# Two transformer blocks on one core: the delta rule's preparation beside the last convolution and the gate, its recurrence beside the indexer's projections

## The chip, the core and the metric

The kernel runs on one core of one Trainium2 chip. The metric is device time in microseconds (us) of one execution. Names of engines: TensorE (PE, with its weight loads as PEld) multiplies matrices, the vector engine (DVE), the scalar engine (ACT) and GpSimd (POOL) work on elements, and SyncE (SP) issues the transfers.

## The reference, cut to what matters

Two layers of a first block, then two layers of a second. The change lies in the first block's attention: a gated delta rule over chunks of 64 tokens in 4 heads, beside sparse attention whose keys are picked by an indexer.

```python
def first_block(x, meta_tokens, w_in, conv_w, a_log, ...):
    h = concatenate([meta, x], axis=1)                  # 16 + 256 tokens, width 1024
    for l in range(DEPTH):                              # DEPTH = 2
        proj = h @ w_in[l]
        dq, dk, dv, dz, db, da, sq, sk, sv, iq, ik, iw = split(proj, SPLIT_POINTS, axis=-1)
        o_dn = deltanet_group(dq, dk, dv, dz, db, da, conv_w[l], ...)
        o_sa = dsa_group(sq, sk, sv, iq, ik, iw, cos, sin, cos_i, sin_i, k_top)
        mix = concatenate([o_dn, o_sa], axis=-1) @ w_out[l]
        ...                                             # layer norm, mixture of experts, layer norm

def deltanet_group(q, k, v, z, b_logit, a_logit, conv_w, a_log, dt_bias, norm_g):
    qkv = silu(causal_dwconv(concatenate([q, k, v], -1), conv_w))
    q, k = l2norm(q), l2norm(k)
    o = chunk_gated_delta_rule(q, k, v, g, beta)
    return o * rsqrt(mean(o * o, -1) + 1e-6) * norm_g * silu(z)

def chunk_gated_delta_rule(q, k, v, g, beta):           # chunks of 64 tokens
    tmat = triangular_solve(eye + lower, eye)           # lower: strict part of k k^T, decayed
    u, w = tmat @ (v * beta), tmat @ (k * beta * exp(gc))
    def step(state, inp):                               # one chunk after the other
        v_new = u_n - w_n @ state
        o_n = qd_n @ state + a_n @ v_new
        return state * exp(gl_n) + kd_n^T @ v_new, o_n

def dsa_group(q, k, v, qi, ki, wi, ...):
    qi, ki = apply_rope(qi), apply_rope(ki)             # the indexer's projections
    score = einsum(relu(qi @ ki^T), wi)
    _, sel = top_k(score, k_top)                        # then attention over the chosen keys
```

## The kernel before

The 272 tokens stand as columns, features as partitions. A projection takes blocks of 128 weight columns: SP fetches two blocks at a time into a ring of four 1 MB buffers, ACT rounds a block to `wh` (line 237), DVE (every fourth time POOL) forms the rest `wl` (line 238), and TensorE makes 24 products of 128x272 for it (lines 245 to 247), into one of three `ps_d` banks. Such a block is called a projection block below.

In each of the two layers `b1_attention` runs, in program order: four projection blocks each for k, q and v with a convolution behind each block (`conv`: one ACT product, three DVE sums of line 395, one tanh, one DVE product of line 398); `squares` and `norms` for the l2 norms; the delta rule's preparation `Delta.pre` for three token tiles t = 2, 0, 1 (16, 128 and 128 tokens), taken in turns by `interleave`; four projection blocks of the gate `zs`; the recurrence `Delta.run` over the tiles; then one block for the indexer's keys `ikT` and four for its queries `iqT`, each with a rotation (`rope`); and then the attention's own projections with the indexer's scores.

`norms` computes the reciprocal roots `rr`: DVE scales the sums of squares (lines 416, 417), POOL raises them to the power -1/2 (line 418), DVE scales again (419, 420). The preparation's first products read `rr` (line 999). It then inverts a triangular matrix by doubling: five levels (three for the 16 tokens), each with a product `LT` by `Tm`, a mask on DVE (`Z`, line 1071), and products that update `Tm` and `U` on DVE (lines 1076, 1077); each product is 8 matmuls of 64x64 (line 1007). The recurrence has for each chunk `wT` by state (line 1144), `u` on DVE (1145), `qd` by state (1148), `kd` by `u` (1154) and the new state on POOL and DVE (1156, 1157). A tile's output is then normed: ACT squares, DVE sums (1169, 1170), POOL takes the power (1171), DVE multiplies (1173), TensorE transposes (1176).

The program is not run in the order of its lines. A scheduler reads the program order as a priority and lays out one fixed sequence for each engine; an engine then works its sequence off in that order, and an instruction that waits holds those behind it. So the gate's blocks already stood among the preparation's products, and the indexer's among the recurrence's.

Of the kernel before, what the change touches and what calls it, by code (L numbers as in the profile page):

```python
# [8 lines left out]
F32 = mybir.dt.float32  # L9
# [4 lines left out]
OP = mybir.AluOpType  # L14
# [3 lines left out]
T1 = 272  # L18
# [328 lines left out]
def interleave(gens):  # L347

    gens = list(gens)
    while gens:  # L350
        for g in list(gens):
            try:
                next(g)
            except StopIteration:
                gens.remove(g)


def yield_from(gen):

    while True:  # L360
        try:
            next(gen)
        except StopIteration as e:
            return e.value


def b1_attention(K, l, mix, st):
# [13 lines left out]
        return ps[:, :T1]  # L381


    def conv(nm, o, tag, *more):
        x = p.tile([128, 4, T1], F32, name=nm + "T", tag=tag)
        for b in range(2):
            wt = K.first.pop(0) if K.first else wcols(K, w, o + 256 * b)
            for j in range(2):
# [7 lines left out]
                th = p.tile([128, T1], F32, name="cvt", bufs=2)  # L396
                S.activation(th, a, AF.Tanh, scale=0.5)
                K.anchor = V.scalar_tensor_tensor(x[:, ci, :], th, 1.0, a, op0=OP.add, op1=OP.mult)
                for at, f in more:
                    if at == ci:  # L400
                        f()
        return x


    def squares(i, x, hs):
        for h in hs:
            sq = p.tile([128, T1], F32, name="l2sq", tag="irel", bufs=3)
            S.activation(sq, x[:, h, :], AF.Square)
            for t in range(3):
                P = TP[t]  # L410
                PE.matmul(pss[:P, t * 8 + i * 4 + h:t * 8 + i * 4 + h + 1], sq[:, TOFF[t]:TOFF[t] + P],
                          c["one"][:, 0:1], start=True, stop=True)
# [6 lines left out]
        V.tensor_scalar(rr[:, :, 0:4], rr[:, :, 0:4], 0.5, None, op0=OP.mult)  # L419
        V.tensor_scalar(rr[:, :, 4:8], rr[:, :, 4:8], 0.5 * 128 ** -0.5, None, op0=OP.mult)  # L420

    kT = conv("k", 512, "kT")

    wsm = p.tile([128, 8, 16], F32, name="wsm", tag="ikT")
    wv = w.rearrange("(k p) n -> p k n", p=128)
# [42 lines left out]

    rr = p.tile([128, 3, 8], F32, name="rr")
    pss = bank(K, "p")  # L470
    hs = [range(2 * i, 2 * i + 2) for i in range(2)]
    qT = conv("q", 0, "qT", *[(1 + i, lambda i=i: squares(0, kT, hs[i])) for i in range(2)])
    load_consts(K, K.pd, 2, nc.sync)
    vT = conv("v", 1024, "vT", *[(i, lambda i=i: squares(1, qT, hs[i])) for i in range(2)], (1, norms))

    load_consts(K, p, 1, nc.sync)
    if l == 0:
# [2 lines left out]
    for i in range(2):  # L480
        nc.sync.dma_start(wik[:, :, i, :], wv[:, :, 4104:4168])
    dt = [Delta(K, l, t, kT, qT, vT, rr, beta, g) for t in range(3)]
    interleave(dt[t].pre() for t in (2, 0, 1))

    zs = p.tile([128, 4, T1], F32, name="zs", tag="kT")
    for b in range(2):
        wt = wcols(K, w, 1536 + 256 * b)
        for j in range(2):
            ps = ws(wt, j * 128)
            th = p.tile([128, T1], F32, name="cvt", bufs=2)  # L490
            S.activation(th, ps, AF.Tanh, scale=0.5)
            V.scalar_tensor_tensor(zs[:, 2 * b + j, :], th, 1.0, ps, op0=OP.add, op1=OP.mult)


    state = None
    for t in (2, 0, 1):
        state = yield_from(dt[t].run(state, zs, mix, t in tiles))
    st["delta"].close()
    K.wb = st["ring"].enter_context(K.tc.tile_pool(name="wringb%d" % l, bufs=RB, side="right"))
    pa = K.pa = st["delta"].enter_context(K.tc.tile_pool(name="attr%d" % l, bufs=1, side="right"))  # L500


    def rope(ps, dst, scale=None):
        raw = p.tile([128, T1], F32, name="rraw", bufs=2)
# [8 lines left out]
        V.tensor_tensor(t2, pr[:, :T1], c["sin"], op=OP.mult)  # L513
        G.tensor_tensor(dst, dst, t2, op=OP.add)

    K.router = router_weights(K, l, K.hp)
    ikT = p.tile([128, T1], F32, name="ikT", tag="ikT")
    rope(ws(wik.rearrange("p k a n -> p k (a n)"), 0), ikT)
    iqT = p.tile([128, 4, T1], F32, name="iqT")
    for b in range(2):  # L520
        wt = wcols(K, w, 3592 + 256 * b)
        for j in range(2):
            rope(ws(wt, j * 128), iqT[:, 2 * b + j, :])
    bias = {2: K.cbmb}
    sqT = p.tile([128, 4, T1], F32, name="sqT", tag="qT")
    skT = p.tile([128, 4, T1], F32, name="skT", tag="vT")
# [1819 lines left out]
```

## Time and profile before

| What | us |
|---|---|
| median of 3 runs | 2074.73 (2064.63 to 2081.65) |
| the profiled execution's own time | 2060.35 |
| its span, from first to last instruction | 2058.5 |
| TensorE busy in the span | 1939.4 (94%) |
| DVE busy | 1067.2 (52%) |
| ACT busy | 768.2 (37%) |
| POOL busy | 364.8 (18%) |
| granted TensorE clock, mean share of 2.4 GHz | 0.969 |

Matmuls are pipelined and their ends are modelled: a matmul of 128x272 is shown with 0.29 us although one starts every 0.125 us, so the idle time of TensorE that the profile shows is a lower bound. The changed part lies in the first layer at about 50 to 170 us of the span and in the second at about 582 to 700 us.

### The profile page before, as it was taken

How to read it: one execution, taken by the hardware profiler on the slowest of the kernel's cores; microseconds unless marked ns; L12 is line 12 of the kernel's file. 1: busy time of each engine (PE TensorE's matmuls, PEld its weight loads, DVE VectorE, ACT ScalarE, POOL GpSimd, SP SyncE). 2: the span in 40 equal slices, each digit the busy share in tenths (PEclk: the TensorE clock that was granted, in tenths of full speed). 3: DMA queues.
4: the chain of work that ended last, by engine and by line, in shares of the span. 5: the costliest groups of instructions: out<-in, count | busy, mean ns of one | idle time of the engine just before them, and what ended most of it. 6: DMA issues, size and time to landing. Idle time of an engine off the chain costs nothing. (4 is left out here: it accounts for less than half of the span.)

```text
span 2058.5 us, 36224 instructions
## 1 busy us (share of the span) xinstructions
PE 1939.4 (94%) x14910; PEld 1526.9 (74%) x14910; DVE 1067.2 (52%) x2112; ACT 768.2 (37%) x1471; POOL 364.8 (18%) x382
## 2 busy tenths in 40 slices
PE   8999999999799998999779999999999999999999
PEld 7888755544588875544358698989888879898987
DVE  6557545322675664322166755555546675555544
ACT  4323432111341343211055344455435434445543
POOL 1325100000122620000010301314200130132410
PEclk9999989999899999999989999999999999999999
DMA  7213279999531346999953442445555244254453
GB/s 227 86 42 122 105 287 383 421 422 422 195 93 63 117 171 274 407 420 423 416 187 124 143 134 93 159 148 164 187 192 160 82 156 152 83 185 144 165 197 110
DMA packets 199339, 414.67 MB, mean 201 GB/s; under 512 B 26024, under 2 KB 147442, under 8 KB 174594
## 3 DMA queue, kind: packets, MB, share of 16 engines
q1 hardware_dynamic: 192230, 410.52, 54.9%
q8 instruction: 119, 1.95, 0.4%
q10 hardware_dynamic: 6940, 1.78, 0.4%
q14 instruction: 50, 0.41, 0.1%
HBM read 411.23 MB, written 1.05 MB: 200 GB/s over the span
## 5 line engine op out<-in xcount | busy, mean ns | idle before, releaser
L238 DVE TENSOR_TENSOR wl<-w,wh 128x1024 fp32r<-128x1024 f32 x329 | 413.0, 1258 | 260.9 <-ACT wh L237 257.5
L237 ACT CAST wh<-w 128x1024 fp32r<-128x1024 f32 x350 | 365.2, 1046 | 424.4 <-PE ps_d L246 251.9
L245 PE MATMUL ps_d<-hh,wh 128*128 128x256 f32 (+1 forms) x1632 | 481.6, 296 | 5.0 <-ACT wh L237 1.9
L247 PE MATMUL ps_d<-hh,wl 128*128 128x256 f32 (+1 forms) x1632 | 476.3, 292 | 0.2
L246 PE MATMUL ps_d<-hl,wh 128*128 128x256 f32 (+1 forms) x1632 | 474.1, 291 | 1.2 <-DVE hl L253 1.2
L245 PEld LDWEIGHTS ps_d<-hh,wh 128*128 128x128 f32 x1632 | 309.4, 190 | 17.3 <-issue 6.7
L247 PEld LDWEIGHTS ps_d<-hh,wl 128*128 128x128 f32 x1632 | 309.9, 190 | 10.1 <-DVE wl L238 6.8
L246 PEld LDWEIGHTS ps_d<-hl,wh 128*128 128x128 f32 x1632 | 309.5, 190 | 6.3 <-DVE hl L253 1.6
L1288 PE MATMUL ps_d<-wb,hg 128*32 128x256 f32 x1600 | 121.2, 389 | 6.3 <-DMA wb<-in_w 6.3
L2313 POOL TENSOR_TENSOR relu<-relu 128x256 f32<-128x256 f32 x64 | 86.7, 1355 | 129.5 <-ACT relu L2312 129.5
L1288 PEld LDWEIGHTS ps_d<-wb,hg 128*32 128x32 f32 x1600 | 59.4, 112 | 50.8 <-DMA wb<-in_w 9.8
L1320 DVE TENSOR_TENSOR yacc<-yacc,ps_c 128x512 f32<-128x512 f32 x56 | 38.5, 688 | 87.7 <-PE ps_c L1317 87.7
L1276 PE MATMUL ps_c<-oh,yp 128*128 128x128 f32 (+1 forms) x640 | 81.4, 280 | 0.0
L1276 PEld LDWEIGHTS ps_c<-oh,yp 128*128 128x128 f32 (+1 forms) x640 | 75.4, 191 | 7.9 <-issue 5.4
L1308 PE MATMUL ps_d<-wb,hid 128*32 128x512 f32 x400 | 70.4, 665 | 6.9 <-ACT hid L1302 6.8
L2267 POOL TENSOR_TENSOR mergedT<-mergedT,tg 128x256 f32<-128x256 f32 x32 | 32.6, 1039 | 231.7 <-DVE tg L2265 231.7
L238 POOL TENSOR_TENSOR wl<-w,wh 128x1024 fp32r<-128x1024 f32 x21 | 50.3, 2395 | 125.6 <-ACT wh L237 116.0
L1292 DVE SCALAR_TENSOR_TENSOR mth<-mth,ps_d 128x256 f32<-128x256 f32 x16 | 6.7, 421 | 125.1 <-ACT mth L1291 125.1
L1291 ACT ACTIVATE mth<-ps_d 128x256 f32<-128x256 f32 x16 | 6.1, 383 | 165.8 <-PE ps_d L1288 165.8
L1317 PE MATMUL ps_c<-ysl,ohT 128*128 128x512 f32 (+1 forms) x140 | 64.9, 603 | 0.0
L2314 ACT CAST hid<-relu 128x256 fp32r<-128x256 f32 x64 | 26.0, 406 | 92.3 <-POOL relu L2313 92.3
L2315 DVE TENSOR_TENSOR hid<-relu,hid 128x256 fp32r<-128x256 f32 x64 | 27.2, 426 | 58.5 <-ACT hid L2314 58.5
(697 smaller groups left out, 3626.9 us busy)
## 6 DMA issues: line engine op xcount, KB each, us to landing
wb<-in_w SPq DMA_DIRECT2D x150, 1024.0 KB, 14.7
w<-in_w_in SPq DMA_DIRECT2D x82, 1024.0 KB, 5.3
w<-in_w SPq DMA_DIRECT2D x42, 1024.0 KB, 19.7
w<-in_w_up SPq DMA_DIRECT2D x32, 1024.0 KB, 5.1
w<-in_w_down SPq DMA_DIRECT2D x32, 1024.0 KB, 4.8
w<-in_w_out SPq DMA_DIRECT2D x16, 1024.0 KB, 4.9
w<-in_w_branch SPq DMA_DIRECT2D x24, 512.0 KB, 3.5
w<-in_cmp_w SPq DMA_DIRECT2D x8, 1024.0 KB
```

The costliest lines, as they stand in the source:

```text
L237: K.nc.scalar.copy(h, x)
L238: eng.tensor_tensor(lo, x, h.bitcast(F32), op=OP.subtract)
L245: PE.matmul(out, a[0], b[0], start=start, stop=False, skip_group_check=True)
L246: PE.matmul(out, a[0], b[1], start=False, stop=False, skip_group_check=True)
L247: return PE.matmul(out, a[1], b[0], start=False, stop=stop, skip_group_check=True)
L1276: PE.matmul(ps[:, (k % 4) * 128:(k % 4) * 128 + 128], K.yp[t][:P, k * 128:(k + 1) * 128], oh[:P, t, :], start=(k == 4 * kk and t == ts[0] ...
L1288: PE.matmul(pu[j * 32:j * 32 + 32, i * 256:i * 256 + 256], hg[:, k, j * 32:j * 32 + 32], wts[i][j][:, k, :], start=(k == 0 and i == 0), st ...
L1308: PE.matmul(ps[q * 32:q * 32 + 32, :], hid[:, j, q * 32:q * 32 + 32], w2t[q][:, j, hf * 512:(hf + 1) * 512], start=(j == 0), stop=(j == 1) ...
L1317: PE.matmul(ps[rows[t]], ohT[:, off:off + P], ysl[:, hf * 512:(hf + 1) * 512], start=True, stop=True)
L1320: V.tensor_tensor(sl, sl, ps[rows[t]], op=OP.add)
L2267: G.tensor_tensor(m, m, tg, op=OP.add)
L2313: G.tensor_tensor(r, r, r, op=OP.mult)
```

## The change

`conv` is split into the tile's creation and a generator `conv_blocks`, which stops after every block. Only the first block of v is projected ahead of the squares of q and of `norms`; the other three and the gate's four then take turns with the preparation, one block for two rounds of it (`weave(..., 2, 1)`; a round is one step of every tile still in work). The recurrence takes turns with the indexer's five projection blocks in the same way. The router's weights are prepared behind the recurrence and not ahead of it. No operation is added or taken away.

```diff
@@ interleave
                 gens.remove(g)
+        yield
@@ b1_attention
-    def conv(nm, o, tag, *more):
+    def conv(nm, o, tag):
         x = p.tile([128, 4, T1], F32, name=nm + "T", tag=tag)
+        return x, conv_blocks(x, o)
+
+    def conv_blocks(x, o):
...
                 K.anchor = V.scalar_tensor_tensor(x[:, ci, :], th, 1.0, a, op0=OP.add, op1=OP.mult)
-                for at, f in more:
-                    if at == ci:
-                        f()
-        return x
+                yield
...
-    qT = conv("q", 0, "qT", *[(1 + i, lambda i=i: squares(0, kT, hs[i])) for i in range(2)])
+    qT, blocks = conv("q", 0, "qT")
+    for i in range(4):
+        next(blocks)
+        if i in (1, 2):
+            squares(0, kT, range(2 * i - 2, 2 * i))
     load_consts(K, K.pd, 2, nc.sync)
-    vT = conv("v", 1024, "vT", *[(i, lambda i=i: squares(1, qT, hs[i])) for i in range(2)], (1, norms))
+    vT, blocks = conv("v", 1024, "vT")
+    next(blocks)
+    squares(1, qT, range(4))
+    norms()
...
-    interleave(dt[t].pre() for t in (2, 0, 1))
-
-    zs = p.tile([128, 4, T1], F32, name="zs", tag="kT")
-    for b in range(2):
...
-    state = None
-    for t in (2, 0, 1):
-        state = yield_from(dt[t].run(state, zs, mix, t in tiles))
...
+    def gate(zs):
+        for b in range(2):
...
+                V.scalar_tensor_tensor(zs[:, 2 * b + j, :], th, 1.0, ps, op0=OP.add, op1=OP.mult)
+                yield
...
+    def index_keys():
+        rope(ws(wik.rearrange("p k a n -> p k (a n)"), 0), ikT)
+        yield
+        for b in range(2):
+            wt = wcols(K, w, 3592 + 256 * b)
+            for j in range(2):
+                rope(ws(wt, j * 128), iqT[:, 2 * b + j, :])
+                yield
+
+    def chunks():
+        state = None
+        for t in (2, 0, 1):
+            state = yield from dt[t].run(state, zs, mix, t in tiles)
+
+    pre = interleave(dt[t].pre() for t in (2, 0, 1))
+    next(pre)
+    next(pre)
+    zs = p.tile([128, 4, T1], F32, name="zs", tag="kT")
+    weave(pre, chain(blocks, gate(zs)), 2, 1)
+    iqT = p.tile([128, 4, T1], F32, name="iqT")
+    ikT = p.tile([128, T1], F32, name="ikT", tag="ikT")
+    weave(chunks(), index_keys(), 2, 1)
...
     K.router = router_weights(K, l, K.hp)
```

What it does to the sequences is seen at three places; the line numbers of the changed kernel are 1 to 19 higher than before.

First, TensorE in layer 0, from the last product of the squares (`l2sq`) to the first that reads `rr`. Before, where the first left-out stretch holds 45 more projection products, and the second the last eleven of them among small products:

```order
L411 MATMUL ps_p<-cst_94,l2sq 16x1
L245 MATMUL ps_d<-hh,wh 128x272
L246 MATMUL ps_d<-hl,wh 128x272
L247 MATMUL ps_d<-hh,wl 128x272
...
L316 MATMUL ps_c<-cst_94,rows 128x68
L976 MATMUL ps_c<-g,cst_94 16x4
...
L999 MATMUL ps_c<-cst_94,rr 128x16 x4
```

Now, where the left-out stretch holds eight more products of the same three kinds:

```order
L412 MATMUL ps_p<-cst_94,l2sq 16x1
L247 MATMUL ps_d<-hh,wl 128x272
L245 MATMUL ps_d<-hh,wh 128x272
L246 MATMUL ps_d<-hl,wh 128x272
...
L1018 MATMUL ps_c<-cst_94,rr 128x16 x7
```

Between the two stood 59 projection products; now there are 11 (in layer 1: 40 before and 9 now).

Second, DVE in layer 0 in the preparation's first two levels (the last figure in `Z_0`, `Tm_1` is the tile t). Before:

```order
L1071 TENSOR_TENSOR Z_2_969<-ps_c_1039,cst2_572 16x64
L1071 TENSOR_TENSOR Z_0_979<-ps_c_1045,cst2_572 128x256
L1071 TENSOR_TENSOR Z_1_996<-ps_c_1055,cst2_572 128x256
L1076 TENSOR_TENSOR Tm_2_970<-Tm_2_970,ps_c_1070 16x64
L1077 TENSOR_TENSOR U_2_971<-U_2_971,ps_c_1065 16x64
```

Now:

```order
L1080 TENSOR_TENSOR Z_0_904<-ps_c_909,cst2_572 128x256
L399 SCALAR_TENSOR_TENSOR cva_995<-ps_d_970,fcol_157,cva_995 128x270
L1080 TENSOR_TENSOR Z_1_921<-ps_c_926,cst2_572 128x256
L399 SCALAR_TENSOR_TENSOR cva_995<-ps_d_970,fcol_157,cva_995 128x269
L238 TENSOR_TENSOR wl_1199<-w_1196,wh_1198 128x1024
L402 SCALAR_TENSOR_TENSOR vT_574<-cvt_1000,cva_995 128x272
L1090 TENSOR_TENSOR Z_2_894<-ps_c_1003,cst2_572 16x64
L1090 TENSOR_TENSOR Z_0_904<-ps_c_1009,cst2_572 128x256
L1090 TENSOR_TENSOR Z_1_921<-ps_c_1019,cst2_572 128x256
L238 TENSOR_TENSOR wl_1303<-w_1196,wh_1302 128x1024
```

Convolution sums and weight splits now stand among the masks and updates of the levels; before, the convolutions were over by then.

Third, POOL in layer 0 around the first whole tile's output norm (`dnst` is the mean square, `iqT` the indexer's queries). Before:

```order
L1156 TENSOR_TENSOR state_1686<-state_1643,ex1_795 128x512
L512 TENSOR_TENSOR iqT_1789<-rraw_1821,cst1_753 128x272
L514 TENSOR_TENSOR iqT_1789<-iqT_1789,rt2_1825 128x272
L1171 TENSOR_TENSOR dnst_1654<-dnst_1654,nhalf_155 128x4
L512 TENSOR_TENSOR iqT_1789<-rraw_1858,cst1_753 128x272
```

Now:

```order
L511 TENSOR_TENSOR iqT_1581<-rraw_1741,cst1_640 128x272
L513 TENSOR_TENSOR iqT_1581<-iqT_1581,rt2_1745 128x272
L1175 TENSOR_TENSOR state_1877<-state_1758,ex1_682 128x512
L1190 TENSOR_TENSOR dnst_1769<-dnst_1769,nhalf_155 128x4
L238 TENSOR_TENSOR wl_1998<-w_1947,wh_1997 128x1024
```

The two rotation operations that stood between the state and the power now stand ahead of both.

## Rows read from the trace of the kernel before

**Rows 1.** The page: busy time of TensorE, share, instructions.
```profile
PE 1939.4 (94%) x14910; PEld 1526.9 (74%) x14910; DVE 1067.2 (52%) x2112; ACT 768.2 (37%) x1471; POOL 364.8 (18%) x382
```

**Rows 2.** Busy time by stretch, both layers: norms, preparation, recurrence.
```profile
core 0: us, PE busy (x) PEld busy (x) DVE busy (x) ACT busy (x) POOL busy (x), PEclk, DMA share, GB/s
50.00:78.00 28.00, 26.14 (x217) 24.84 (x216) 19.57 (x54) 10.10 (x20) 8.89 (x3) 0.94 0.40 123
78.00:132.00 54.00, 52.44 (x872) 45.16 (x867) 32.62 (x80) 11.38 (x22) 13.27 (x14) 0.94 0.16 49
132.00:170.00 38.00, 35.87 (x263) 31.78 (x263) 15.56 (x23) 9.10 (x15) 17.09 (x16) 0.96 0.17 50
582.00:612.00 30.00, 27.98 (x212) 27.08 (x210) 18.62 (x52) 11.05 (x23) 6.54 (x2) 0.89 0.34 105
612.00:664.00 52.00, 51.57 (x879) 44.92 (x878) 31.46 (x83) 11.51 (x23) 13.15 (x13) 1.00 0.20 63
664.00:700.00 36.00, 34.48 (x265) 30.65 (x264) 16.87 (x23) 9.83 (x18) 19.74 (x17) 1.00 0.27 88
```

**Rows 3.** Timeline of DVE at `norms`: start, length, line, operation [idle before].
```profile
56.25 0.17 DVE L416 TENSOR_SCALAR rr<-ps_p 128x16 f32<-128x16 f32 x1 [1.03 <-PE ps_p L411]
62.04 0.17 DVE L419 TENSOR_SCALAR rr<-rr 128x12 f32<-128x12 f32 x1 [3.66 <-POOL rr L418]
...
591.68 0.17 DVE L416 TENSOR_SCALAR rr<-ps_p 128x16 f32<-128x16 f32 x1 [1.06 <-PE ps_p L411]
597.26 0.17 DVE L419 TENSOR_SCALAR rr<-rr 128x12 f32<-128x12 f32 x1 [3.81 <-POOL rr L418]
```

**Rows 4.** Timeline of POOL: the two powers of `norms`; a weight split; an output norm.
```profile
48.77 2.39 POOL L238 TENSOR_TENSOR wl<-w,wh 128x1024 fp32r<-128x1024 f32 x1 [12.73 <-ACT wh L237]
56.63 5.38 POOL L418 TENSOR_TENSOR rr<-rr,nhalf 128x24 f32<-128x24 f32 x1 [5.47 <-DVE rr L417]
...
146.71 0.77 POOL L514 TENSOR_TENSOR iqT<-iqT,rt 128x272 f32<-128x272 f32 x1 [0.46 <-DVE dnst L1170]
147.44 1.03 POOL L1171 TENSOR_TENSOR dnst<-dnst,nhalf 128x4 f32<-128x4 f32 x1
...
593.06 4.17 POOL L418 TENSOR_TENSOR rr<-rr,nhalf 128x24 f32<-128x24 f32 x1 [0.85 <-DVE rr L417]
```

**Rows 5.** Timeline of TensorE: projection products, and the wait in layer 1.
```profile
52.03 0.29 PE L246 MATMUL ps_d<-hl,wh 128*128 128x272 f32 x1
52.16 0.29 PE L247 MATMUL ps_d<-hh,wl 128*128 128x272 f32 x1
...
600.14 0.47 PE L999 MATMUL ps_c<-cst,rr 16*128 16x16 f32 x4 [2.02 <-DVE ex L980]
```

**Rows 6.** Busy time of two stretches at half the clock, as in Rows 2.
```profile
91.70:98.50 6.80, 6.80 (x108) 6.12 (x108) 2.15 (x7) 0.37 (x1) 0.00 (x0) 0.50 0.01 2
600.30:607.10 6.80, 6.80 (x33) 6.76 (x32) 2.82 (x17) 1.08 (x3) 0.00 (x0) 0.50 0.44 149
```

**Rows 7.** Timeline of TensorE in the preparation: a level's product twice; a projection product.
```profile
97.10 1.06 PE L1007 MATMUL ps_c<-U,Z 64*64 64x64 f32 x16
...
101.76 0.39 PE L246 MATMUL ps_d<-hl,wh 128*128 128x272 f32 x1
...
104.19 0.63 PE L1007 MATMUL ps_c<-U,Z 64*64 64x64 f32 x16
```

**Rows 8.** Waits of TensorE in the recurrence, layer 0 and layer 1: total, times, longest.
```profile
PE ps_c L1176 <- DVE don L1173: 2.1, 2, 1.9
...
PE ps_c L1176 <- DVE don L1173: 1.5, 2, 0.8
```

**Rows 9.** Groups of DVE operations, 50 to 170 us: busy, mean ns, idle before.
```profile
L238 DVE TENSOR_TENSOR wl<-w,wh 128x1024 fp32r<-128x1024 f32 x10 | 13.7, 1371 | 2.5 <-ACT wh L237 1.8 <-PE ps_d L247 0.6
L395 DVE SCALAR_TENSOR_TENSOR cva<-ps_d,fcol,cva 128x270 f32<-128x270 f32 x5 | 2.5, 492 | 0.1
L398 DVE SCALAR_TENSOR_TENSOR vT<-cvt,cva 128x272 f32<-128x272 f32 x4 | 1.7, 428 | 0.0
```

**Rows 10.** The page's transfers: count, size, median us from issue to landing.
```profile
w<-in_w_in SPq DMA_DIRECT2D x82, 1024.0 KB, 5.3
```

More of the change, by code (lines that the diff above doesn't have):

```diff
@@ L420, in norms @@
         V.tensor_scalar(rr[:, :, 4:8], rr[:, :, 4:8], 0.5 * 128 ** -0.5, None, op0=OP.mult)
-    kT = conv("k", 512, "kT")
+    kT, blocks = conv("k", 512, "kT")
+    run(blocks)
     wsm = p.tile([128, 8, 16], F32, name="wsm", tag="ikT")
@@ L470, in b1_attention @@
     pss = bank(K, "p")
-    hs = [range(2 * i, 2 * i + 2) for i in range(2)]
-    qT = conv("q", 0, "qT", *[(1 + i, lambda i=i: squares(0, kT, hs[i])) for i in range(2)])
+    qT, blocks = conv("q", 0, "qT")
[3 more added lines that the diff above has]
+            squares(0, kT, range(2 * i - 2, 2 * i))
     load_consts(K, K.pd, 2, nc.sync)
-    vT = conv("v", 1024, "vT", *[(i, lambda i=i: squares(1, qT, hs[i])) for i in range(2)], (1, norms))
+    vT, blocks = conv("v", 1024, "vT")
+    next(blocks)
+    squares(1, qT, range(4))
+    norms()
     load_consts(K, p, 1, nc.sync)
@@ L482, in b1_attention @@
     dt = [Delta(K, l, t, kT, qT, vT, rr, beta, g) for t in range(3)]
-    interleave(dt[t].pre() for t in (2, 0, 1))
-    zs = p.tile([128, 4, T1], F32, name="zs", tag="kT")
-    for b in range(2):
[L487 to L492, printed above, removed]
-    state = None
-    for t in (2, 0, 1):
-        state = yield_from(dt[t].run(state, zs, mix, t in tiles))
-    st["delta"].close()
-    K.wb = st["ring"].enter_context(K.tc.tile_pool(name="wringb%d" % l, bufs=RB, side="right"))
-    pa = K.pa = st["delta"].enter_context(K.tc.tile_pool(name="attr%d" % l, bufs=1, side="right"))
+    def gate(zs):
+        for b in range(2):
+            wt = wcols(K, w, 1536 + 256 * b)
+            for j in range(2):
+                ps = ws(wt, j * 128)
+                th = p.tile([128, T1], F32, name="cvt", bufs=2)
+                S.activation(th, ps, AF.Tanh, scale=0.5)
+                V.scalar_tensor_tensor(zs[:, 2 * b + j, :], th, 1.0, ps, op0=OP.add, op1=OP.mult)
+                yield
     def rope(ps, dst, scale=None):
@@ L514, in rope @@
         G.tensor_tensor(dst, dst, t2, op=OP.add)
-    K.router = router_weights(K, l, K.hp)
[L517 to L523, printed above, removed]
+    def index_keys():
[3 more added lines that the diff above has]
+            wt = wcols(K, w, 3592 + 256 * b)
+            for j in range(2):
+                rope(ws(wt, j * 128), iqT[:, 2 * b + j, :])
[12 more added lines that the diff above has]
+    weave(chunks(), index_keys(), 2, 1)
+    st["delta"].close()
+    K.wb = st["ring"].enter_context(K.tc.tile_pool(name="wringb%d" % l, bufs=RB, side="right"))
+    pa = K.pa = st["delta"].enter_context(K.tc.tile_pool(name="attr%d" % l, bufs=1, side="right"))
+    K.router = router_weights(K, l, K.hp)
     bias = {2: K.cbmb}
```

## The prediction

> **What bounds the kernel now.** I read the page first: TensorE is busy for 94% of the span [rows 1], so a change that only moves work can win no more than TensorE's idle time and slow clock in the stretches that it touches. The second view is therefore the busy time by stretch [rows 2], three stretches in each layer: the norms with the last convolutions (50 to 78 us and 582 to 612 us), the preparation (to 132 and 664) and the recurrence (to 170 and 700). Length less TensorE's busy time is 1.86, 1.56 and 2.13 us in layer 0 and 2.02, 0.43 and 1.52 us in layer 1: 9.5 us idle. The granted clock is 0.94, 0.94, 0.96 and 0.89, 1.00, 1.00. Each share that is missing is time at 1.2 instead of 2.4 GHz, and if all work doubled its time there, (1 - share) by length would be the loss: 1.7, 3.2, 1.5, 3.3, 0 and 0 us, 9.7 us in all. Idle and clock together are 19.2 us, under 1% of 2060.35 us. Third come the timelines around the waits, to see who is late. In both layers it is the same chain: DVE scales the sums of squares, POOL takes the power in 5.38 and 4.17 us [rows 4], and DVE stands idle for 3.66 and 3.81 us until it can scale again [rows 3], with all that stands behind it in its sequence. TensorE runs out of work shortly afterwards: 2.02 us at 600.14 in layer 1 [rows 5], and a clock at half for the 6.8 us that follow [rows 6]. In the recurrence it waits 2.1 and 1.5 us for the normed outputs [rows 8].
>
> **The change part by part.** Nothing is added or removed, so each term is a wait that gets shorter or longer.
>
> *The wait for the reciprocal roots gets longer.* From the first scaling to the end of the second DVE and POOL take about 56.25 to 62.3 and 591.68 to 597.5 us, 6.0 and 5.8 us [rows 3]. This chain keeps its length, but the work that TensorE has meanwhile shrinks from 59 and 40 projection products to 11 and 9 (counted from the sequences). A product starts 0.13 us after the one before it [rows 5], so the cover is 1.4 and 1.2 us. TensorE then idles for 4.6 and 4.6 us. Of the second I take 4.2 us, since in layer 1 the power itself lasts 1.2 us less [rows 4] and the 5.8 us hold a delay by a convolution's product. That is 8.8 us against the 3.9 us that are idle in these stretches now: **+4.9 us**. Bounds: 0, if what stands now behind the roots is late anyway, and +8.3, if besides the clock stays low in layer 0 for 6.8 us, as it does in layer 1, and not for half of that (3.4 us at half the pace cost 1.7 us, in each layer at most).
>
> *The preparation gets more to do between its levels.* Three projection blocks of v now stand in it. Of its 2.0 us of idle time I let 1.5 go. Its slow stretch at 91.7 to 98.5 us [rows 6] comes after products of 64x64 and 16x16 with few projection products among them; in layer 1 the same sequence keeps the full clock [rows 2], so it is a matter of little, and with more large products among the small ones I expect it to go. What it is worth is read from like work: sixteen products of a level take 1.06 us at half the clock and 0.63 at full [rows 7], so 40% of 6.8 us, 2.7 us. Together **-4.2 us**; bounds 0 and -5. The Trainium skill, page "TensorE: Matmul & The Clock Gate", section Terms, prices a throttled time by the share of the clock that is missing, which would be half of it, 3.4 us. The row shows 40% for these small products, and by the page the sum would be 0.7 us lower.
>
> *The recurrence.* Each output norm holds TensorE while ACT, DVE, POOL and DVE follow each other. In layer 0 POOL takes the power at 147.44 us, behind a rotation of 0.77 us that started 0.46 us after its mean square was there or about to be [rows 4]; that rotation now stands ahead of the state's scaling, and about 0.7 us go. The projection products between a tile's last product and its transposes are 25, 19, 21 and 20 before and 24, 20, 24 and 24 now, 7 more by 0.13 us: 0.9 us. Together 1.6 of the 3.6 us that are waited there [rows 8]. The clock's loss in layer 0 is 1.5 us, and it comes right behind the longest of these waits; I let it go with the wait. **-3.1 us**; bounds 0 and -5.1.
>
> *More switching.* A projection product right behind small products takes 0.39 us and not 0.29 [rows 7, 5], and I take as much again for the step back: 0.2 us for each stretch of projection products. Their number grows from 45 to 48 and from 44 to 48 (counted in the sequences): **+1.4 us**; bounds 0 and +2.8.
>
> *What I cost at nothing.* The three convolutions that move into the preparation bring DVE nine sums of 0.49 us and three products of 0.43 us in each layer [rows 9], 5.7 us on an engine that is busy for 32.62 of 54 and 31.46 of 52 us there [rows 2]; the cover is TensorE's larger work, 72 products or 9 us, and what it costs without that cover is the first rival. ACT, at 11.38 of 54 us, has room for the six operations that come with them. SP now fetches v's second pair of blocks behind the constants and the indexer's key weights; a fetch lands in 5.3 us [rows 10], and the pair is first split at 48.77 us [rows 4], while in layer 0 the fetches around 32 us are over by 40. Should the pair be late, DVE and POOL would hold for what is missing of 5.3 us, once a layer. The router's weights move from the preparation to the recurrence with two short DVE operations and one split; DVE is busy for 15.56 of 38 us there [rows 2].
>
> The sum is 4.9 - 4.2 - 3.1 + 1.4 = **-1.0 us** on the profiled execution's 2060.35 us. That execution is 14.4 us below the median of the three runs, 2074.73 us, and faster than each of them, so I carry the difference to the median: **2073.7 us**, no change that can be told.
>
> **The rivals.** *DVE falls behind in the preparation (slower).* Among the masks and updates of the first two levels there are now eight sums, three products and two splits in layer 0, 8 x 0.49 + 3 x 0.43 + 2 x 1.37 = 8.0 us [rows 9]. Each level is a chain from TensorE to DVE and back. From the point at which TensorE has fewer projection products between two levels than DVE has foreign work, each of these operations lengthens the chain, up to 8 us a layer, and the gains of the preparation and the recurrence stay out: 16 + 4.9 + 1.4 = 22.3 us, 2097 us. For it: 2 to 9 products, 0.3 to 1.1 us, often stand between two groups of a level. Against it: DVE is busy for only 60% of that stretch. 0.10.
>
> *All waits go (faster).* The idle time and the slow clock of all six stretches are filled, and the wait for the roots finds other work: 9.5 + 9.2 - 1.4 = 17.3 us with the clock's loss in the preparation taken at 2.7, 2057 us. The Trainium skill, page "Perfetto Trace Analysis", section Optimization Strategy, says that regimes which differ in the engine most in demand may gain from being interleaved; that is this rival. The trace bears it out in part: DVE is busy for 60% in the preparation and 41% in the recurrence [rows 2], but the regimes were already mixed by the scheduler, and the sequence leaves 11 and 9 products of cover at the roots. 0.15.
>
> *The change does little of what it says.* The scheduler had mixed these parts before, the stretches are again full of TensorE's work, and all terms are small: 2075 us. For it: only 9.5 us are idle over 238 us of these stretches. 0.30.
>
> **How the numbers follow.** My forecast has 0.45, and the time is its own: 2073.7 us, rounded to 2073. The range must hold the last rival and the forecast with its bounds: 4.9 + 1.7 + 1.7 + 2.8 = +11 us when no gain comes and -9 when the gains are whole and the wait costs nothing, 2066 to 2086. The three runs lie 7 to 10 us on either side of their median, and the faster rival lies at 2057, so I take 2053 to 2088; the slower rival and the faster one's far half are left out. About 1%, 20 us, is what a measurement of this kernel can tell from no change. Faster by more needs all of the second rival and a low draw: 0.10. Slower by more needs the first: 0.08. Within 1%: 0.82.
>
> **What would show it.** The roots: TensorE idle for about 4 to 5 us ahead of its first product that reads `rr`, in both layers, with DVE idle just as long until POOL's power ends; if it is under 2 us, that term fails. The preparation: a granted clock of 1.00 from the first to the last level, in both layers. The recurrence: waits for the normed output below 1 us each. DVE: idle time ahead of the masks that still ends with TensorE's products; if TensorE waits for masks and updates for over 3 us a layer, the first rival is at work. I am wrong in the whole if the time leaves 2053 to 2088 us, above all if half a clock's stretch of more than 7 us follows the roots, which no row before shows.

## The result, and the profile after

The changed kernel is slower: a median of 2083.93 us of 13 runs (2071.98 to 2092.71), against 2074.73 us of 13 runs of the kernel before (2064.63 to 2085.25). The ratio is 1.0067, with a 95% interval of 1.0043 to 1.0091 (the two medians alone would give 1.0044); a second series gave 1.0077 (1.0044 to 1.0110). The forecast was 2073 us and no change. The time lies inside the range of 2053 to 2088 us and by the prediction's bound of 1% it is no change; but the loss is clear of its interval in both series, and a small gain was forecast.

The page first: TensorE's share is what it was, and it is busy for 25 us longer with the same 14910 products [rows 1].

```profile
PE 1964.2 (94%) x14910; PEld 1545.0 (74%) x14910; DVE 1062.8 (51%) x2112; ACT 769.5 (37%) x1471; POOL 365.0 (17%) x382
```

The same products take longer when the clock is lower. This is the busy time by stretch of the changed kernel, in the columns of [rows 2]; the column to read is PEclk.

```profile
50.00:78.00 28.00, 25.49 (x207) 23.80 (x205) 12.98 (x52) 8.13 (x18) 7.73 (x6) 0.70 0.18 56
78.00:132.00 54.00, 52.93 (x811) 45.88 (x808) 31.95 (x75) 10.10 (x18) 10.61 (x9) 0.91 0.20 60
132.00:170.00 38.00, 37.62 (x295) 33.06 (x294) 16.76 (x27) 11.39 (x19) 19.58 (x18) 1.00 0.28 84
582.00:612.00 30.00, 24.71 (x197) 24.04 (x195) 18.79 (x56) 10.55 (x21) 6.99 (x3) 0.89 0.26 82
612.00:664.00 52.00, 51.34 (x826) 43.77 (x822) 30.60 (x82) 10.63 (x22) 10.58 (x11) 0.90 0.21 63
664.00:700.00 36.00, 35.60 (x286) 32.34 (x286) 17.98 (x28) 10.71 (x17) 15.58 (x14) 1.00 0.20 60
```

Norms in layer 0 went from 0.94 to 0.70 (in layer 1 they stayed at 0.89), the preparation from 0.94 and 1.00 to 0.91 and 0.90; the recurrence of layer 0 went from 0.96 to 1.00. Where the clock is at 1.2 GHz is seen in the windows that hold exactly these stretches, in the same columns: in layer 0 17.1 us from 53.1 and 10.2 us in the levels (before: 6.8 us [rows 6]), in layer 1 6.8 us at the roots, as before, and 10.2 us in the levels, where there was none.

```profile
53.10:70.20 17.10, 14.59 (x69) 14.18 (x70) 4.62 (x25) 2.82 (x7) 4.53 (x1) 0.50 0.20 61
87.30:97.50 10.20, 10.20 (x128) 8.63 (x126) 3.60 (x9) 1.81 (x3) 2.36 (x1) 0.50 0.33 105
602.70:609.50 6.80, 5.24 (x26) 5.18 (x27) 4.25 (x13) 0.21 (x1) 1.39 (x1) 0.50 0.39 113
626.60:636.80 10.20, 10.20 (x129) 8.89 (x125) 4.51 (x11) 1.75 (x3) 0.00 (x0) 0.50 0.34 105
```

Before, layer 0 had 3.4 us at the roots and 3.4 us in the recurrence:

```profile
67.80:71.20 3.40, 3.40 (x15) 3.40 (x16) 1.66 (x11) 0.64 (x2) 0.00 (x0) 0.50 0.37 130
149.70:153.10 3.40, 3.40 (x18) 3.18 (x17) 2.47 (x3) 0.62 (x1) 1.49 (x1) 0.50 0.17 58
```

A second profile of the changed kernel has layer 0 as here. In layer 1 it has one long stretch at the roots and none in the levels:

```profile
595.50:616.00 20.50, 16.63 (x81) 16.18 (x80) 8.16 (x24) 2.62 (x6) 6.47 (x2) 0.50 0.17 52
```

What TensorE did ahead of the stretch in layer 0 stands in its timeline (start, length, line, operation, idle before):

```profile
49.86 0.28 PE L247 MATMUL ps_d<-hh,wl 128*128 128x272 f32 x1
49.99 1.30 PE L412 MATMUL ps_p<-cst,l2sq 128*128 128x1 f32 x12
51.22 0.28 PE L316 MATMUL ps_c<-cst,rows 68*128 68x68 f32 x1
...
51.85 0.36 PE L996 MATMUL ps_c<-g,cst 128*128 128x4 f32 x2
52.08 0.37 PE L245 MATMUL ps_d<-hh,wh 128*128 128x272 f32 x1
52.29 0.29 PE L246 MATMUL ps_d<-hl,wh 128*128 128x272 f32 x1
52.41 0.63 PE L412 MATMUL ps_p<-cst,l2sq 128*128 128x1 f32 x6
52.98 0.47 PE L247 MATMUL ps_d<-hh,wl 128*128 128x272 f32 x1
...
64.41 0.89 PE L1018 MATMUL ps_c<-cst,rr 16*128 16x16 f32 x7 [2.51 <-DVE ex L999]
...
604.26 0.79 PE L1018 MATMUL ps_c<-cst,rr 16*128 16x16 f32 x6 [5.29 <-DVE ex L999]
```

From 49.99 to 53.1 us it is almost only products with one or four columns of output, and three projection products. The clock falls at 53.1 us, 8.8 us before TensorE runs out of work at 61.9 us and waits for rr. The wait comes on top: 2.51 and 5.29 us, in sum twice the 3.9 us that were idle in the two norm stretches before (in the second profile 2.51 and 3.87 us).

**A measure that leaves the rest of the program out.** In each layer I take the time from the keys' first square to the first product of `memx` into `ps_p`, behind the attention heads: the same work in every kernel. Before:

```profile
38.89 0.83 PE L411 MATMUL ps_p<-cst,l2sq 128*128 128x1 f32 x7
...
218.40 0.60 PE L1675 MATMUL ps_p<-cst,memx 128*128 128x128 f32 x4
...
572.55 0.61 PE L411 MATMUL ps_p<-cst,l2sq 128*128 128x1 f32 x5
...
743.00 0.60 PE L1675 MATMUL ps_p<-cst,memx 128*128 128x128 f32 x4
```

And the changed kernel:

```profile
38.31 0.63 PE L412 MATMUL ps_p<-cst,l2sq 128*128 128x1 f32 x6
...
223.40 0.60 PE L1694 MATMUL ps_p<-cst,memx 128*128 128x128 f32 x4
...
578.92 0.50 PE L412 MATMUL ps_p<-cst,l2sq 128*128 128x1 f32 x4
...
757.57 0.60 PE L1694 MATMUL ps_p<-cst,memx 128*128 128x128 f32 x4
```

That is 179.51 + 170.45 = 349.96 us before and 185.09 + 178.65 = 363.74 us now: 13.8 us more, where I had forecast 1.0 less. The two profiles are 32.2 us apart in all; the rest lies in code that the change does not touch, and the second profile of the changed kernel (2074.2 us, stretches of 363.1 us) shows that it is no part of it. In the second block, between the same two products, the first profile and then the second have these windows:

```profile
1651.00:1678.80 27.80, 26.65 (x111) 18.91 (x112) 18.77 (x42) 5.59 (x11) 8.06 (x9) 0.63 0.13 39
```

```profile
1648.00:1668.30 20.30, 19.11 (x110) 13.88 (x110) 17.42 (x40) 5.66 (x11) 7.04 (x8) 0.92 0.17 53
```

One kernel, one piece of code, 27.8 or 20.3 us, with the clock at 0.63 or 0.92.

### The profile page after: what moved, and what is told of

It reads as the page before. It is cut to its first block, busy times and chain, and to the rows that moved or that the text cites. A ratio compares the mean times of both kernels' runs of the same rounds, so it can differ in the third digit from the quotient of the medians.

```text
span 2090.7 us, 36208 instructions
## 1 busy us (share of the span) xinstructions
PE 1964.2 (94%) x14910; PEld 1545.0 (74%) x14910; DVE 1062.8 (51%) x2112; ACT 769.5 (37%) x1471; POOL 365.0 (17%) x382
## 5 line engine op out<-in xcount | busy, mean ns | idle before, releaser
L245 PE MATMUL ps_d<-hh,wh 128*128 128x256 f32 (+1 forms) x1632 | 486.6, 299 | 4.6 <-ACT tg L2272 1.9
L247 PEld LDWEIGHTS ps_d<-hh,wl 128*128 128x128 f32 x1632 | 314.1, 193 | 9.5 <-DVE wl L238 6.8
```

Of the source, the lines that this page charges most:

```text
L245: PE.matmul(out, a[0], b[0], start=start, stop=False, skip_group_check=True)
L247: return PE.matmul(out, a[1], b[0], start=False, stop=stop, skip_group_check=True)
```

## The experiments

Each kernel was timed in five rounds beside the kernel before on the same chip. For each the table has how many of v's blocks stand ahead of the preparation, the sum of the two stretches above (one profile each), the half-clock stretches from the keys' squares to the last chunk in both layers, counted by half their length, and the ratio to the kernel before. The first block of s1 is that of the kernel before, so it is a second profile of it.

| kernel | v ahead | stretches, us | half-clock, halved | ratio (95%) |
|---|---|---|---|---|
| before | 4 | 350.0 | 10.2 | |
| the change, two profiles | 1 | 363.7, 363.1 | 22.2, 23.9 | 1.0067, 1.0077 |
| x1 v's move alone | 1 | 365.1 | 25.6 | 1.0078 (1.0050 to 1.0106) |
| e4 recurrence as before | 1 | 366.2 | 27.3 | 1.0092 (1.0055 to 1.0130) |
| e8 squares apart | 1 | 356.6 | 13.7 | 1.0055 (1.0026 to 1.0083) |
| e5 half roots | 1 | 354.7 | 17.1 | 1.0096 (1.0066 to 1.0125) |
| x5 both mends | 1 | 355.1 | 17.1 | 1.0059 (1.0033 to 1.0085) |
| e7 roots of k only | 1 | 351.1 | 10.2 | 1.0094 (1.0059 to 1.0129) |
| e10 two ahead | 2 | 355.2 | 15.4 | 1.0057 (1.0035 to 1.0080) |
| e11 three ahead | 3 | 354.0 | 11.9 | 1.0055 (1.0034 to 1.0076) |
| e2 v behind the squares | 4 | 348.9 | 6.8 | 1.0057 (1.0033 to 1.0081) |
| e1 v ahead, weaves kept | 4 | 349.1 | 8.5 | 1.0042 (1.0013 to 1.0071) |
| e3 recurrence only | 4 | 347.0 | 8.5 | 1.0030 (0.9997 to 1.0063) |
| s1 before, later code shifted | 4 | 349.0 | 10.2 | 1.0010 (0.9981 to 1.0038) |
| e6 e1 with half roots | 4 | 350.0 | 11.9 | 1.0003 (0.9976 to 1.0029) |
| x6 before with half roots | 4 | 339.4 | 1.7 | 1.0000 (0.9974 to 1.0027) |
| x7 x6 with e3's weave | 4 | 345.4 | 10.2 | 1.0010 (0.9986 to 1.0035) |

Every kernel with fewer than four of v's blocks ahead is slower by 0.55 to 0.96%; those with four lie between 0.00 and 0.57%.

**First theory: the wait for the roots, with the clock behind it.** Rival: the weave in the preparation by itself. Four kernels, the first with

```diff
-    next(blocks)
-    squares(1, qT, range(4))
-    norms()
+    for i in range(4):
+        next(blocks)
+        if i < 2:
+            squares(1, qT, range(2 * i, 2 * i + 2))
+        if i == 1:
+            norms()
...
-    weave(pre, chain(blocks, gate(zs)), 2, 1)
+    weave(pre, gate(zs), 2, 1)
```

> All four blocks of v stand ahead of the preparation again, with the norms behind the second, as before the change; gate and indexer stay woven. Between the squares and rr there are 59 and 40 projection products again, not 11 and 9. If the loss is the wait at the roots (with the clock that follows it) or v's blocks among the levels, the time is that of the kernel before, 2074 us, ratio 0.998 to 1.002, and TensorE idles for under 2 us ahead of rr in each layer. If the gate's woven blocks or the indexer's cost it, or the time follows the clock by chance, it stays at 2080 us or more.

2076.39 us against 2069.47. The stretches are those of the kernel before, 349.1 us, and so is TensorE's wait ahead of rr, 0.23 us in layer 0 and, in layer 1, as in [rows 5]:

```profile
603.17 0.37 PE L1021 MATMUL ps_c<-cst,rr 16*128 16x16 f32 x4 [2.02 <-DVE ex L1002]
```

The median came less than half of the way back, between what the two theories said.

The second is the kernel before with the weave of the recurrence alone:

```diff
-    for t in (2, 0, 1):
-        state = yield_from(dt[t].run(state, zs, mix, t in tiles))
...
+    weave(chunks(), index_keys(), 2, 1)
```

> The kernel before, with the indexer's five blocks woven into the recurrence and nothing else. By the stretches of the two traces the recurrence has gained 1.5 us, so 2071 to 2074 us and a ratio of 0.997 to 1.000 if all of the loss lies ahead of it. If the weave of the recurrence takes part in the loss, 2078 us or more.

2078.78 us against 2069.47: by the time the second case, but with an interval that reaches to no change. The stretches are 2.9 us shorter, as the forecast had it, 2.8 of them in layer 0. In the median the gain does not show.

The third and the fourth shorten the wait. In `norms(i)` of e5 the power takes 12 columns, the keys' behind the third block of q; e7 calls `norms()` there once and takes all 24 from the keys' sums:

```diff
+        if i == 2:
+            norms(0)
...
-    norms()
+    norms(1)
```

> The change, but the power is taken in two halves: the keys' roots as soon as the keys' squares are summed, and only the queries' behind the first block of v, so that POOL needs about 2.2 us less between the squares and rr. If the wait for the roots is the cause, TensorE's idle time ahead of rr (2.5 us in layer 0, 5.3 us in layer 1) falls by about 2 us in each layer and the time by 4 to 6 us, to 2078 to 2080 us. If the preparation's own weave is the cause, 2082 us or more and half-clock stretches of about 10 us in the levels as in the changed kernel.

> The change, with the queries' roots left out: all 24 roots are taken from the keys' sums of squares, behind the third block of q, so that nothing waits for the power behind the first block of v; the queries' squares are still summed but not read. This takes the wait at the roots away whole and leaves the weaves. If the wait with the clock behind it is the cause, 2072 to 2076 us, ratio 0.998 to 1.001 to the kernel before, and the levels of the preparation keep the full clock. If the weave in the preparation costs by itself (slow clock and switching, 5.9 us by the two traces), 2079 us or more.

2092.18 and 2089.86 us against 2069.47: ratios no better than the change's own, so by the median the first theory falls. The rival fares no better: the stretches got shorter, by 9.0 and 12.6 us, and at half the clock in the levels e5 has 6.8 us and e7 3.4. In layer 0 another wait stands in the place of the old one, and the clock is at half there for 13.7 us (e5) and 17.1 us (e7). TensorE's timeline in e5, ahead of the squares of the last heads:

```profile
52.89 1.14 PE L412 MATMUL ps_p<-cst,l2sq 128*128 128x1 f32 x6 [1.59 <-ACT l2sq L409]
```

and in e7, ahead of the gate logits' products:

```profile
56.37 0.59 PE L998 MATMUL ps_c<-g,cst 128*128 128x4 f32 x2 [2.26 <-DVE lcol L318]
```

With three projection blocks gone from this place, the next in line is late there: ACT's squares, or DVE's copy. In layer 1, e7 has no slow clock at all, and its stretch is 167.8 us, against 178.6 in the change and 170.4 before:

```profile
580.00:748.00 168.00, 164.38 (x1751) 147.55 (x1750) 111.68 (x270) 58.92 (x119) 64.75 (x53) 1.00 0.29 95
```

So in the stretch of layer 1 the wait does matter, and the slow clock went with it; the median does not show it.

**Is it the clock, and whose?** The listing of each run has its span and granted clock. The span times the share that was not granted is the clock lost in it: a mean of 75.5 us in 35 runs of the kernel before, 85.3 us in the 12 of the changed kernel beside them, of mean spans of 2067.7 and 2083.2 us. Counted so, 9.8 of the 15.5 us are clock and 5.7 us are not (a slight overcount: over the 35 runs the span grows by 0.83 us for each us of lost clock). The changed kernel again:

> The changed kernel itself, as the base of this group, with the granted clock of every run. The runs of the kernel before in the first group split into a span at half the clock, counted by half its length (75 us of 2068 on average, the span less that 1993 us). The changed kernel is expected at 1996 to 1997 us and 84 to 88 us of lost clock: two thirds of its loss is the clock. If the loss is in the work and the waits alone, the lost clock is 75 us as before.

Close to what was expected: 85.3 us of lost clock, and a span less lost clock of 1997.9 us, 0.9 us more. The next adds three scalings of a tile on the way into the second block of the kernel before:

```diff
+        for _ in range(3 if t == 0 and not hasattr(K, "moved") else 0):
+            V.tensor_scalar(x, x, 1.0, None, op0=OP.mult)
+        K.moved = True
```

> The kernel before, with three extra scalings by 1.0 of one tile (0.75 us each) on the path into the second block, where TensorE idles for 11.6 us anyway: no instruction of the first block changes, the second block's code is the same and stands some 2.2 us later. If the clock that is lost depends only on what TensorE does, the lost clock stays at 75 us and the time grows by 2 us. If it depends on when the same code arrives (the second block lost 13 us of clock in two profiles and 30 to 42 us in four others, with the same instructions), the lost clock moves by 6 us or more, either way.

Lost clock 79.3 us, 3.8 more, time 2074.16 against 2071.51 us: neither of the two values expected, so it stays open how far the time at which the later code arrives moves the median.

e8 is the change with two of the four heads' squares earlier:

```diff
+        if i == 3:
+            squares(1, qT, range(2))
...
-    squares(1, qT, range(4))
+    squares(1, qT, range(2, 4))
```

> The change, with the sums of squares of the queries' first two heads ahead of v's first block, among large products, so that only two heads' squares stand with the gate logits' small products ahead of the roots. The wait for the roots is the same, 11 and 7 projection products stand in it. If the four heads' squares in one place let the clock fall at 53 us for 17 us, that stretch is gone or at most 7 us long and the lost clock falls by 5 us or more from the changed kernel's, the time to about 2079 us. If the wait itself or the small products behind it let it fall, nothing changes: 2082 us or more.

The stretch of 17.1 us at half the clock in layer 0 is gone; one of 6.8 us starts at 61.1 us:

```profile
53.00:61.10 8.10, 5.77 (x48) 5.48 (x47) 2.71 (x14) 3.53 (x8) 3.48 (x1) 1.00 0.01 2
61.10:67.90 6.80, 5.41 (x27) 5.34 (x28) 2.67 (x12) 0.22 (x1) 1.04 (x1) 0.50 0.44 136
```

The lost clock falls to 79.2 us, as expected, but the rest of the span grows by 2.6 us to 2000.5, and 2083.52 us is a smaller gain than expected; its interval overlaps that of the change. e6 is e1 with the two halves of e5:

```diff
+        if i == 2:
+            norms(0)
...
         if i == 1:
-            norms()
+            norms(1)
```

> v's four blocks ahead of the preparation as before the change, gate and indexer woven, and the power taken in two halves, the keys' early. Span less lost clock: 1993 us with v ahead, some 3 us less by the shorter wait in each layer, 1989 to 1991 us. If the lost clock is what the sequence around the squares makes it, it stays at 75 to 80 us and the time is 2066 to 2072 us, level with the kernel before or a little faster. If the shift of the later code decides, the lost clock may come out at 90 us or more and the time above 2080 us.

2068.58 us against 2071.51, lost clock 74.1 us: level with the kernel before, near the first case. The rest is 1993.5 us and not the 1989 to 1991 us expected of the shorter wait.

**Which part of the change.** x1 moves v's three blocks, with the queries' squares and `norms` behind v's first block as in the change, and leaves out both other weaves; e4 is the change without the recurrence's weave.

```diff
+    weave(pre, blocks, 2, 1)
...
-    weave(pre, chain(blocks, gate(zs)), 2, 1)
...
-    weave(chunks(), index_keys(), 2, 1)
+    run(gate(zs))
+    run(chunks())
...
+    run(index_keys())
```

> Of the change only that three of v's blocks move from ahead of the roots into the preparation; the gate's blocks stand behind the preparation and the indexer's behind the recurrence in program order, as before. If the moved blocks are the cause (v ahead again gave back 11 us of lost clock in block 1's profile), this is as slow as the whole change: lost clock 82 to 88 us, 2080 to 2088 us, and the clock at half from 53 us. If the weaves are, 2074 us or less.

2089.16 us, ratio 1.0078, lost clock 92.0 us against 80.6 in the kernel before beside it: the whole loss, and a little more than expected. At the roots the picture is that of the change in layer 0 and that of its second profile in layer 1; in the levels there are 6.8 us in each layer:

```profile
53.30:70.40 17.10, 14.59 (x70) 14.18 (x70) 4.74 (x24) 2.82 (x7) 4.53 (x1) 0.50 0.21 62
87.40:94.20 6.80, 6.80 (x81) 5.87 (x78) 2.44 (x6) 0.96 (x2) 0.00 (x0) 0.50 0.23 61
589.20:609.70 20.50, 16.62 (x81) 16.18 (x80) 7.84 (x25) 2.90 (x7) 6.48 (x2) 0.50 0.17 52
626.80:633.60 6.80, 6.80 (x99) 5.72 (x94) 3.92 (x10) 0.87 (x1) 0.00 (x0) 0.50 0.44 145
```

```diff
-    weave(chunks(), index_keys(), 2, 1)
+    run(chunks())
...
+    run(index_keys())
```

> The change without the weave of the recurrence: the indexer's blocks stand behind it in program order. If the recurrence's weave gives 1.5 us, as its stretch shows, 2085 to 2089 us; if it takes part in the loss, 2082 us or less.

2093.91 us, more than either case had it. The stretches are 2.5 and 3.1 us longer than in the two profiles of the change, but the recurrence is not what made them so: from the first product that reads `vT`, behind the levels, to `memx` it is 213.4 us in e4 and 213.2 and 213.0 us in the change. The difference lies ahead of it, where e4's profile has more slow clock: 27.3 us counted by half against 22.2 and 23.9. A gain of the recurrence's weave in its own place is seen in e3, not here.

For x5, e5 with e8's lines:

```diff
+        if i == 2:
+            norms(0)
+        if i == 3:
+            squares(1, qT, range(2))
...
-    squares(1, qT, range(4))
-    norms()
+    squares(1, qT, range(2, 4))
+    norms(1)
```

> The change with both mends: the keys' roots early, and the squares of the queries' first two heads ahead of v's first block. If the wait (6 us of the span less lost clock) and the squares in one place (6 us of lost clock) are separate causes that add up, 2074 to 2079 us. If a shorter wait only moves the small products closer together, as the halves alone did (98 us of lost clock), the lost clock stays above 85 us and the time above 2082 us.

2086.69 us against 2073.95, 89.5 us of lost clock: the second case, the two mends do not add up.

And for x6, on the kernel before, with `norms(i)` of e5:

```diff
-    qT = conv("q", 0, "qT", *[...])
-    vT = conv("v", 1024, "vT", *[...], (1, norms))
+    qT = conv("q", 0, "qT", *[...], (2, lambda: norms(0)))
+    vT = conv("v", 1024, "vT", *[...], (1, lambda: norms(1)))
```

> The kernel before with the power in two halves, the keys' early, and nothing else. The wait there is 3.7 us on DVE and 1.8 us on TensorE in each layer, so up to 3 us: 2067 to 2071 us, ratio 0.998 to 1.000. If the denser work lets the clock fall more, 2074 us or more.

2072.96 us against 2073.95: the time lies between the two cases, the ratio is 1.0000. The stretches are 10.6 us shorter, and the slow clock in them, counted by half, went from 10.2 to 1.7 us; the median is not shorter. In this profile the second block lost 31.8 us of clock, in that of the kernel before 13.3.

**What in the move.** e2 puts `run(blocks)` behind `norms()`, so that v's other three blocks come ahead of the preparation; e10 and e11 leave two and three blocks ahead, with the squares two by two:

```diff
     squares(1, qT, range(4))
     norms()
+    run(blocks)
...
-    weave(pre, chain(blocks, gate(zs)), 2, 1)
+    weave(pre, gate(zs), 2, 1)
```

> Norms behind v's first block as in the change, with the squares of the queries' four heads close together; but v's other three blocks stand right behind, ahead of the preparation, so that 62 and 43 projection products lie between squares and rr, and the gate logits' small products come behind them. If what lets the clock fall is that too little large work lies between the small products, the lost clock is as before (75 to 81 us), the stretch behind rr at most 7 us long and the time 2072 to 2076 us. If the four heads' squares in one place do it, the clock falls at 53 us and the time is 2080 us or more.

```diff
-    next(blocks)
-    squares(1, qT, range(4))
+    for i in range(2):
+        next(blocks)
+        squares(1, qT, range(2 * i, 2 * i + 2))
     norms()
+    next(blocks)    # in e11 alone
```

> Two of v's blocks ahead of the roots with the squares two by two behind them as before the change, two in the preparation; 9 and 15 projection products between squares and rr. If the missing large work between squares and rr lets the clock fall, it falls here too, for 10 us or more ahead of the levels, and the time is 2080 us or more. If the squares in one place do it, or the three blocks in the levels, it is half way or better: 2074 to 2079 us.

> As the last, and v's third block behind the norms and ahead of the preparation: 35 and 16 projection products between squares and rr, one block of v in the levels. By the missing large work layer 0 is as before the change and layer 1 as in the last: 2075 to 2079 us. By the blocks in the levels: within 2 us of the kernel before.

2082.14, 2081.83 and 2083.16 us against 2072.06. In the stretches of layer 0 the places at half the clock are those that the theory of the missing large work has. In e2, with the four heads' squares close together but 62 projection products behind them, the clock stays at full until 66.0 us:

```profile
53.00:66.00 13.00, 11.12 (x89) 10.43 (x87) 8.30 (x17) 5.15 (x8) 6.33 (x2) 1.00 0.36 106
66.00:72.80 6.80, 6.37 (x29) 6.16 (x29) 3.28 (x18) 2.40 (x6) 0.20 (x1) 0.50 0.31 109
```

In e10, with the squares apart but 9 products ahead of rr, it falls for twice as long:

```profile
58.30:72.00 13.70, 11.95 (x56) 11.29 (x55) 5.90 (x26) 2.28 (x6) 2.75 (x1) 0.50 0.11 40
```

At the roots e11 has 3.4 us in layer 0, as before the change, and 10.2 us in layer 1, as e10; it has 10.2 us more in the levels of layer 1. But the medians do not follow the stretches: e2's are 348.9 us and its time is 10 us above the kernel before, where this theory had 2072 to 2076 us, and e11 lies above both of its cases. In e2's profile the second block lost 41.8 us of clock (its stretches at half the clock, counted by half), in that of the kernel before 13.3, with the same instructions: behind `memx` of layer 1 every profile has the same 8643 products of TensorE.

The last joins the diffs of x6 and e3:

```diff
+    qT = conv("q", 0, "qT", *[...], (2, lambda: norms(0)))
+    vT = conv("v", 1024, "vT", *[...], (1, lambda: norms(1)))
...
+    weave(chunks(), index_keys(), 2, 1)
```

> The kernel before with the two parts that gained in their own stretches: the keys' roots early (10.5 us less in the two changed stretches of its profile, but no gain in the median) and the indexer's blocks woven into the recurrence (2.7 to 2.9 us less, twice). If the stretches' gains reach the end, 2060 to 2066 us, ratio 0.994 to 0.997. If the clock of the later, unchanged code takes them back, as with each of the two alone, 2070 us or more and a ratio of 0.999 to 1.003.

2069.14 us against 2067.77: by the ratio the second case. Nor did the stretches' gains add up: 345.4 us is 6.0 more than in x6, with 17.1 us at half the clock in the levels of layer 1. No kernel of these beats the one before.

## Why the prediction was wrong, step by step

*The step that failed* is the one on the clock. I let the slow clock of the preparation go (2.7 of the 4.2 us), with "more large products among the small ones", and bounded the slow clock at the roots by 6.8 us in layer 0. It went the other way: in all from 10.2 us, counted by half, to 22.2 and 23.9 us in the two profiles of the change. That is 11.9 and 13.7 us more, and the stretches grew by 13.8 and 13.1. At the roots, both layers together, it went from 5.1 to 11.9 and 18.8 us; in the levels, from 3.4 to 10.2 and 5.1. The sign that I had named, more than 7 us at half the clock behind the roots, came in a stronger form: 17.1 us (layer 0) and, in the second profile, 20.5 us (layer 1), and they begin ahead of the first product of rr.

The three blocks were not only cover for the wait: with them the squares, the gate logits' products and the first products of rr stood apart, without them they stand together, and there the clock fell. x1, which moves them without the other weaves, has the whole loss; e1 and e3, which keep them, have the stretches of the kernel before. I had counted the missing products (59 to 11, 40 to 9) and priced them as idle time alone. A ceiling of 19.2 us on the gain was right; that nothing of like size could come on top was not asked. Which part of the place lets the clock fall is shown only in part: e2, e8 and e10 speak for the missing large products in layer 0, e7 and x6 show that with a shorter wait slow clock goes, too, and in layer 1 the two are not told apart.

*The wait for the roots* was sized about right, 7.8 us of idle time (6.4 in the second profile) against 8.8, but for mixed reasons. In layer 0 the 11 products ran at 1.2 GHz and covered more; in layer 1 DVE's scaling added 2.1 us that I had not priced (below). The 2.02 us that TensorE waited in layer 1 before [rows 5] were not the roots' alone: they end with DVE's copy `ex` at 599.85 us, 2.3 us behind the scaling of rr, and between the two DVE had a weight split and convolutions. That this wait is the whole loss is not borne out: without it e7 is as slow by the median, though its stretches are shorter by 12.6 us.

*The preparation:* -4.2 us forecast. The granted clock should have been 1.00 from the first to the last level; it was 0.91 and 0.90. Of the 2.0 us of idle time 1.5 should have gone; in the same windows 1.7 are left. The Trainium skill, page "Perfetto Trace Analysis", section Optimization Strategy, which I had as a rival, says that stretches with different engines in demand may gain from being interleaved. Here v's convolutions in the levels gained nothing, the indexer in the recurrence 2.9 us in e3's stretches.

*The recurrence:* -3.1 us forecast, and this term held. The waits for the normed output fell from 3.6 [rows 8] to 2.3 us, 1.3 for the forecast 1.6, each below 1 us, as said:

```profile
PE ps_c L1195 <- DVE don L1192: 1.2, 2, 0.8
```

```profile
PE ps_c L1195 <- DVE don L1192: 1.1, 2, 0.6
```

The 3.4 us at half the clock at 149.7 us are gone, in e3 as in the change, 1.7 us by half for the forecast 1.5. One row was misread on the way: the 0.46 us in [rows 4] are POOL's idle time before the rotation, which began 0.07 us after the mean square was done; the power still came 0.8 us behind it, so the 0.7 us stand.

*The switching* (+1.4 us) is not told apart from the clock. *The rival with DVE falling behind* is not at work: DVE is busy for 31.95 of 54 us in the preparation, 32.62 before, and no long wait of TensorE there names a mask or an update. The forecast's sum was 2073.7 us, which rounds to 2074 and not to 2073.

*Open.* By the median, kernels whose stretches agree within 2.2 us differ by up to 0.9% (e2 and e7 against e6), so the stretches do not explain the medians of the others. In single profiles the difference lies in the clock of the second block, whose code is the same; whether a kernel meets that by chance or by when its later code starts, one profile for each and s1 do not decide. e1's 0.42% and e3's 0.30% are of this kind, too. Of the change itself it is shown that its stretch grew and by what; how much of its 0.67 and 0.77% comes from there, and how much from the second block, is not.

## What to carry to other kernels

Large matrix products that stand among small ones may be worth more there than the wait that they cover: before moving them, list what is left in the place, and price that place at half the clock, too, not only as idle time. Judge a change of under 1% by the length of the changed stretch between the same two products, beside the median, and do not take one for the other; two profiles of one kernel were 16.5 us apart, all but 0.6 us of it outside that stretch.

## What was not expected of the hardware

DVE waits for POOL on some operations. In layer 1 POOL began a weight split right behind the power, and the scaling of rr that DVE started 0.06 us later took 2.30 us, not 0.17 [rows 3], until POOL was done:

```profile
601.75 2.34 POOL L238 TENSOR_TENSOR wl<-w,wh 128x1024 fp32r<-128x1024 f32 x1
601.81 2.30 DVE L420 TENSOR_SCALAR rr<-rr 128x12 f32<-128x12 f32 x1 [3.75 <-POOL rr L419]
604.03 0.15 DVE L421 TENSOR_SCALAR rr<-rr 128x12 f32<-128x12 f32 x1
```

It is so in both profiles of the change and in x1. The Trainium skill, page "SBUF — State Buffer", section "SBUF: two separate sides", describes an exclusive lock on a port pair that DVE and GpSimd share, which one instruction holds for its whole length. The trace agrees: DVE's scaling ends at 604.11 us, 0.02 us behind POOL's split. The split stood there because the change moved it behind the power (before, it began at 589.83 us, ahead of it): in a queue, what comes next matters to the neighbour, too.
